# A decoder block on one core: the SSD chunks' buffers, queue and state, one ring of split weights, and y_a's operand

## The chip, the cores and the metric

The kernel runs on one core of a Trainium2 chip. The metric is the device time of one execution in microseconds, the median of several runs. The kernel before took 2039.7 us (three runs: 2036.38, 2039.7 and 2045.04).

In what follows PE is the tensor engine (matmuls), DVE the vector engine, ACT the scalar engine, POOL the GpSimd engine and SP the sync engine, which here only issues DMAs. PSUM is the memory that matmuls write, in banks; SBUF is the memory that the other engines work in.

## The reference

One layer, a sequence of 1024 positions, model width 1024, all in float32:

```
u  = rmsnorm(h)
P  = u @ W_in          # 1024 x 10272: gate_a, gate_s, B_a, C_a, v_a, z, xBC, dt
y_a = (B_a * causal_dwconv3(C_a * v_a)) @ W_a_out
xBC = silu(causal_dwconv4(xBC) + b)          # x (2048), B and C (4 groups x 128 each)
y  = SSD(x, dt, B, C) + d_skip * x           # 32 heads of 64, state 128, chunks of 128
y_s = group_rmsnorm(y * silu(z)) @ W_s_out   # 4 groups of 512
h  = h + (sigmoid(gate_a) * y_a + sigmoid(gate_s) * y_s) @ W_o
v  = rmsnorm(h)
h  = h + (silu(causal_dwconv3(v @ W_1) + b) * (v @ W_3)) @ W_down
out = rmsnorm(h)
```

For one group and one chunk of 128 positions, SSD is: a masked product inside the chunk (C Bᵀ times a decay, times x·dt), plus C times the state at the chunk's start times a decay, and then state = state × (decay of the whole chunk) + Bᵀ(x·dt·decay to the end). There are 4 groups with 8 chunks each, so 32 chunks, and the state is carried over 8 of them.

## The kernel before, in words

**Products.** Each float32 operand is split into a high and a low part (`split`, L146: ACT copies the high part, DVE or POOL subtracts for the low part), and a product adds high×high, high×low and low×high. A product (L248) has 12 matmuls of 128×512. Two column tiles of a weight make a `Pair` (L261), which computes its 2×2 block product with seven products in place of eight. They have fixed names by their operand: b11, b21 (`first`), t1, t2, t3, t4, b22 (`second`); t1 to t4 are sums and differences of weight tiles formed on POOL (L292, L293, L304, L310). The results are put together on DVE (u2, u3 and the drains, L302 to L314).

**Buffers.** Tiles come from rings; an instruction that writes a tile waits until the last reader of the ring's oldest tile is done. Here: raw weights (`load`, L156, SP's queue) 3; split weights `w` 11, and a second ring `wx` of 4 for t4 and b22; t1 to t3 in a ring `t2` of 3; `big` 14 tiles of 128×2048, the operands among them. PSUM has four banks `mm` and four banks `sd`. The products t1, t4 and b22 and all tiles of the SSD take `sd` banks in turn, so whatever is allocated four places later takes the same bank.

**The scratch of `fill_second`** (L207), which transposes rows of the activation and forms the five remaining combinations, are two tiles per row block; they come from the ring `wx`.

**SSD chunks.** `ssd_chunk` (L617) is a generator with eight stages; every finished product advances a clock (`tick`, L324), and the stages of chunk number s are due at 11 + 6s plus the offsets in STAGES (L54). So a chunk starts every six products, between the projections of x, B, C, z, the convolution mixer and the gates. Its steps, with the lines of the profile:

- m: decays loaded through ACT's queue, then exponentials on ACT (L639, L640)
- in: x, B, C of the chunk loaded from DRAM by SP's queue (L633), two buffers
- px, pb, pc (L645, L647, L649): transposes of x and B, and BᵀC, each in a bank of its own; xd, xe, bk and cb are drawn from them (L651, L658, L666, L668); POOL multiplies x by d_skip in place (L662)
- eb, zt: decays and silu(z) loaded by ACT's queue (L680 for zt, one buffer)
- pd, po, pst (L687, L694, L700): the product inside the chunk, C times the state, and the state's increment
- POOL scales the state in place (L702), DVE adds pd (L706), DVE multiplies po by its decay (L708), POOL adds that (L709), DVE adds pst to the state (L716), DVE multiplies by the gate in place, over x (L718)
- ACT squares (L721) and writes y to DRAM out of the buffer of x (L722), DVE sums (L723, L725); PE sums over partitions (pn, L728), DVE forms the mean (yss, L730), POOL the power (yr, L734)

Afterwards `ta_half` (L793) loads y_a's operand through the ring of raw weights in pieces of two tiles and splits them; `y_a` (L807) follows.

**Order.** A scheduler of the framework lays out each engine's instructions in one list ahead of time; each engine runs its list strictly in order. Where an instruction waits, all behind it on that engine wait too, DMA issues on the queues of SP and ACT among them.

Of the kernel before, what the change touches and what calls it, by code (L numbers as in the profile page):

```python
# [15 lines left out]
P = 128  # L16
# [17 lines left out]
NRAW, NW, NWX, NBIG, NB4, NC2, NT2, NROW = 3, 11, 4, 14, 3, 6, 3, 6  # L34
# [19 lines left out]
STAGES = LOAD_M, LOAD_IN, DECAY, TRANS, LOAD_Z, DIAG, SQUARES, NORM = -9, -8, -6, -4, -3, 0, 3, 6  # L54
# [11 lines left out]
def tile_block(  # L66
# [58 lines left out]
    def w2(name, tag="w", dt=F32R):  # L125
        return wp.tile([P, HALF], dt, tag=tag, name=name, bufs=NW if tag == "w" else NWX)
# [24 lines left out]
    def wsplit(v, name, eng=None, tag="w"):  # L151
        hi, lo = w2(f"h_{name}", tag), w2(f"l_{name}", tag)
        split(v, hi, lo, eng)
        return hi, lo
# [5 lines left out]

    ident = const([P, P], "ident")
# [45 lines left out]
    def fill_second(A, vts, name):  # L207

        pts, sls, sm = [], [], []
        for v, t in vts:  # L210
            pts.append(transposed(v, f"{name}{t}", mm_tile))
            sls.append(slice(t * P, (t + 1) * P))

        def piece(nm, i, f):
            return f(f"{nm}_{name}{vts[i][1]}").rearrange("p (k t) -> p k t", k=4)

        def wx(nm):
            return w2(nm, "wx", F32)
# [4 lines left out]
        def whole(c, i, f):  # L223
            o = piece(c, i, f)
# [5 lines left out]
        a11 = [whole("a11", i, c2) for i in both]  # L230
# [5 lines left out]
        s3 = [piece("s3", i, wx) for i in both]  # L236
# [4 lines left out]
        a12 = [whole("a12", i, wx) for i in both]  # L241
# [19 lines left out]
    class Pair:  # L261
# [26 lines left out]
        def operands(self):  # L288
            name, b11 = self.name, self.r1[:, :HALF]
            self.r2 = load(self.src2, f"2{name}")  # L290
            self.t1, self.t2 = t2(f"t1{name}"), t2(f"t2{name}")
            pool.tensor_tensor(self.t1, self.r2[:, :HALF], b11, op=ALU.subtract)  # L292
            pool.tensor_tensor(self.t2, self.r2[:, HALF:], self.t1, op=ALU.subtract)  # L293

        def second(self, d2):
            name, m1, d1 = self.name, self.m1, self.d1
            b21, t1, tb = self.r1[:, HALF:], self.t1, self.t2
            b12, b22 = self.r2[:, :HALF], self.r2[:, HALF:]
# [4 lines left out]
            t3 = t2(f"t3{name}")  # L303
            pool.tensor_tensor(t3, b22, b12, op=ALU.subtract)  # L304
            p = self.prod("s3", t3, "t3")
# [44 lines left out]
    halves = [slice(0, HALF), slice(HALF, SEQ)]  # L350
# [78 lines left out]
    for j in range(0, 4, 2):  # L429
        for t in (4 + j, 5 + j):  # L430
            u_norm(t)
        fill_second(U, [(xs[t], t - 4) for t in (4 + j, 5 + j)], "u")
# [182 lines left out]
    states, stats = {}, {}  # L615

    def ssd_chunk(s):  # L617
# [15 lines left out]
        sp.dma_start(inp, xd_[g][:, 0:6, ts])  # L633
# [45 lines left out]
        zt = ssp.tile([P, 4, P], F32, tag="z", name=f"zt{nm}", bufs=1)  # L679
# [21 lines left out]
        if st is not None and c < NCH - 1:  # L701
            pool.tensor_tensor(  # L702
                heads(st), heads(st),
                cdb[:, q, hsl, cc : cc + 1].to_broadcast([P, HG, HD]), op=ALU.mult,
            )
# [4 lines left out]
        if c < NCH - 1:  # L710
            if st is None:
                st = ssp.tile([P, HALF], F32, tag="st", name=f"st{g}", bufs=1)
                act.copy(st, pst)
                states[g] = st
            else:
                dve.tensor_tensor(st, st, pst, op=ALU.add)  # L716

        dve.tensor_tensor(xt, xt, zt, op=ALU.mult)  # L718
        yield
        sq = eb  # L720
        act.activation(sq, xt.rearrange("p j l -> p (j l)"), AF.Square)  # L721
        act.dma_start(yd[g, c // 4][:, :, hts], xt)  # L722
# [506 lines left out]
```

## Time and profile before

| | |
|---|---|
| median of three runs | 2039.7 us |
| profiled execution | 2035.02 us |
| its span, first to last instruction | 2033.3 us |
| mean granted clock of PE | 0.981 |
| busy: PE, DVE, POOL, ACT | 1933.0, 1390.5, 1309.6, 909.9 us |
| HBM traffic | 166 GB/s over the span |

By stage: the head to 110 us; projections without SSD to 250; projections with the SSD chunks beside them to 960; y_a and the rest of the mixer to 1325; the norm ahead of the FFN to 1420; the up projections of the FFN to 1795; the down projections to the end.

How to read the rows: a line such as `DVE st L716 <- POOL st L702: 68.4, 17, 11.6` says that DVE, at line 716 writing the tile st, sat idle 68.4 us in all, 17 times, at most 11.6 us, until POOL's instruction of line 702 was done. Names have their numbers left out: st is the state of any group, `in` the buffer of x, B and C. A row with `SPq` or `ACTq` is a DMA issue on that engine's queue. The clock column is the share of full speed that PE was granted.

### The profile page before, as it was taken

The numbers are of one execution on the slowest core, as the hardware profiler recorded it, in microseconds if no ns is written. First come the engines' busy times: TensorE is split into PE (matmuls) and PEld (weight loads), VectorE is DVE, ScalarE is ACT, GpSimd is POOL, SyncE is SP. The second block draws the span as 40 slices with busy tenths as digits, with TensorE's granted clock in tenths as the row PEclk, the third lists the DMA queues.
The fourth block names the chain that finished last, engine by engine and source line by source line (L and its number), as shares of the span: only waits on it lengthen the run. The fifth ranks groups of instructions, "written<-read, shape, count | busy, mean of one in ns | idle before, by whom it ended". The sixth has DMA issues, their size and how long they took to land.

```text
span 2033.3 us, 25995 instructions
## 1 busy us (share of the span) xinstructions
PE 1933.0 (95%) x8978; PEld 1578.5 (78%) x8978; DVE 1390.5 (68%) x1588; ACT 909.9 (45%) x1687; POOL 1309.6 (64%) x959
## 2 busy tenths in 40 slices
PE   7899999989999999998999999998999999999998
PEld 6788877767778778776787888876888888887886
DVE  8765996767778767766775724367876677784445
ACT  5364447536636655444333423354433333343434
POOL 7777877766777678676545322367888777753452
PEclk9999999999999999999999999998999999999999
DMA  4252234535444544477998555542332244467664
GB/s 150 62 174 99 104 126 147 169 121 158 161 121 132 184 140 151 109 231 241 325 342 322 194 183 181 166 156 73 130 109 99 91 151 148 156 224 272 211 193 155
DMA packets 184339, 338.46 MB, mean 166 GB/s; under 512 B 19472, under 2 KB 91920, under 8 KB 183184
## 3 DMA queue, kind: packets, MB, share of 16 engines
q1 hardware_dynamic: 122512, 266.53, 39.3%
q10 hardware_dynamic: 61696, 70.27, 11.6%
q8 instruction: 71, 1.16, 0.2%
q14 instruction: 60, 0.49, 0.1%
HBM read 247.34 MB, written 89.41 MB: 166 GB/s over the span
## 4 chain that ended last, share of the span: by engine, by line
PE 63%; DMA 13%; DVE 9%; POOL 7%; issue 5%; ACT 3%; SPq 0%; ACTq 0%; POOLq 0%; DVEq 0%
PE so L255 7%; PE pt2up L255 3%; PE pt4up L255 3%; DMA wd<-in_w_down 3%; PE pt3up L255 3%; PE pb22up L255 3%; PE pb11up L255 3%; PE pt1up L255 3%; PE pb21up L255 3%; PE d L1022 2%; PE d L1024 2%; PE d L1023 2%; PE ya L255 2%; PE pb22xb L255 1%; PE pt4xb L255 1%
## 5 line engine op out<-in xcount | busy, mean ns | idle before, releaser
L536 DVE SCALAR_TENSOR_TENSOR cv<-xbc,scw,cv 128x1024 f32<-128x1024 f32 x72 | 131.9, 1855 | 15.2 <-ACT cv L532 15.2
L639 ACT ACTIVATE m<-m,tk 128x128 f32<-128x128 f32 x256 | 79.2, 390 | 112.1 <-DMA m<-acd 96.1
L536 DVE SCALAR_TENSOR_TENSOR fcv<-fci,fcw,fcv 128x1024 f32<-128x1024 f32 x44 | 77.8, 1769 | 31.4 <-ACT fcv L532 31.4
L149 POOL TENSOR_TENSOR l_ws<-raw_ws,h_ws 128x512 fp32r<-128x512 f32 x32 | 44.9, 1405 | 77.4 <-issue 29.2
L148 ACT CAST h_ws<-raw_ws 128x512 fp32r<-128x512 f32 x64 | 38.5, 621 | 85.5 <-PE so L255 59.6
L255 PE MATMUL so<-yh,h_ws 128*128 128x512 f32 x256 | 70.0, 396 | 4.4 <-ACT h_ws L148 4.4
L149 DVE TENSOR_TENSOR l_ws<-raw_ws,h_ws 128x512 fp32r<-128x512 f32 x32 | 28.0, 880 | 64.0 <-PE so L255 35.0
L255 PE MATMUL so<-yl,h_ws 128*128 128x512 f32 x256 | 69.5, 393 | 0.0
L255 PE MATMUL so<-yh,l_ws 128*128 128x512 f32 x256 | 68.6, 390 | 0.0
L658 ACT ACTIVATE xe<-px,tk 128x64 f32<-128x64 f32 x256 | 55.9, 329 | 25.6 <-DVE xd L651 25.5
L149 POOL TENSOR_TENSOR l_wo<-raw_wo,h_wo 128x512 fp32r<-128x512 f32 x24 | 34.3, 1432 | 50.8 <-ACT h_wo L148 24.9
L292 POOL TENSOR_TENSOR t1up<-raw_2up,raw_1up 128x512 f32<-128x512 f32 x22 | 32.0, 1455 | 53.8 <-DMA raw_2up<-in_w_up 38.5
L716 DVE TENSOR_TENSOR st<-st,pst 128x512 f32<-128x512 f32 x24 | 16.5, 686 | 71.0 <-POOL st L702 68.7
L255 PEld LDWEIGHTS so<-yh,h_ws 128*128 128x128 f32 x256 | 47.8, 189 | 15.4 <-ACT h_ws L148 5.9
L718 DVE TENSOR_TENSOR in<-in,zt 128x512 f32<-128x512 f32 x32 | 44.9, 1404 | 18.8 <-POOL in L709 16.4
L255 PEld LDWEIGHTS so<-yl,h_ws 128*128 128x128 f32 x256 | 48.6, 190 | 10.3
L255 PEld LDWEIGHTS so<-yh,l_ws 128*128 128x128 f32 x256 | 48.3, 189 | 10.2
L1010 DVE TENSOR_TENSOR fcv<-fcv,h 128x1024 f32<-128x1024 f32 x22 | 39.8, 1811 | 23.2 <-ACT fcv L1009 23.2
L148 ACT CAST h_wo<-raw_wo 128x512 fp32r<-128x512 f32 x48 | 29.6, 622 | 56.8 <-PE wo L896 26.8
L895 PE MATMUL wo<-l_wo,mh 128*128 128x512 f32 x128 | 51.2, 400 | 3.2 <-DVE l_wo L149 3.2
L669 DVE TENSOR_TENSOR m<-m,cb 128x1024 f32<-128x1024 f32 x32 | 53.2, 1662 | 0.4
L896 PE MATMUL wo<-h_wo,ml 128*128 128x512 f32 x128 | 50.8, 398 | 0.0
(1060 smaller groups left out, 6664.4 us busy)
## 6 DMA issues: line engine op xcount, KB each, us to landing
m<-acd ACTq DMA_DIRECT2D x32, 512.0 KB, 4.5
raw_ws<-in_w_s_out SPq DMA_DIRECT2D x32, 512.0 KB, 4.7
ssd_in<-cv ACTq DMA_DIRECT2D x24, 512.0 KB, 2.7
in<-ssd_in SPq DMA_DIRECT2D x32, 384.0 KB, 3.9
raw_wo<-in_w_o SPq DMA_DIRECT2D x24, 512.0 KB, 3.5
wd<-in_w_down SPq DMA_DIRECT2D x22, 512.0 KB, 6.1
td<-wd SPq DMA_DIRECT2D x44, 256.0 KB, 4.6
raw_1up<-in_w_up SPq DMA_DIRECT2D x22, 512.0 KB, 3.4
```

The source lines that it names most:

```text
L148: act.copy(hi, v)
L149: (eng or pool).tensor_tensor(lo, v, f32(hi), op=ALU.subtract)
L255: pe.matmul(ps, wt[:, k, :], ct[:, k, :], start=(start and n == 0), stop=(stop and n == 11),)
L536: dve.scalar_tensor_tensor(cv, ci[:, j : j + SEQ], w[:, j : j + 1], cv, op0=ALU.mult, op1=ALU.add)
L639: act.activation(m[:, h, :], m[:, h, :], AF.Relu, bias=a)
L658: act.activation(xe[:, hc], px[:, hc], AF.Copy, scale=tk[:, 2, cc, q, g * HG + h : g * HG + h + 1],)
L669: dve.tensor_tensor(m, m, cb.unsqueeze(1).to_broadcast([P, HG, P]), op=ALU.mult)
L718: dve.tensor_tensor(xt, xt, zt, op=ALU.mult)
L895: pe.matmul(pss[t], mh, wl, start=False, stop=False)
L896: pe.matmul(pss[t], ml, wh, start=False, stop=k == NK - 1)
L1022: pe.matmul(ps, aa[0][:, ts], bb[0], start=k == 0, stop=False)
L1023: pe.matmul(ps, aa[0][:, ts], bb[1], start=False, stop=False)
```

## The change

It has three parts.

1. *SSD tiles.* The load of x, B, C moves from SP's queue to ACT's and is due one product earlier, at the same one as the load of m (LOAD_IN −9). The multiply by the gate writes into zt instead of the buffer of x, and the square and the write to DRAM read zt, which gets a second buffer. pb and pc share one bank. The state is no longer scaled in place ahead of its add: after each add POOL scales the new state by the next chunk's decay into a tile of its own, sn, and the next add reads sn.
2. *Rings.* One ring of 13 split weights takes the place of 11 and 4. t3 is formed with t1 and t2, in `operands`. The scratch of `fill_second` comes from a small pool (at the head) or is the row block's own two halves (ahead of the FFN).
3. *y_a's operand* is loaded into a tile of 128×2048 of its own in two pieces, no longer through the ring of raw weights.

```diff
-NRAW, NW, NWX, NBIG, NB4, NC2, NT2, NROW = 3, 11, 4, 14, 3, 6, 3, 6
+NRAW, NW, NBIG, NB4, NC2, NT2, NROW = 3, 13, 14, 3, 6, 3, 6
...
-STAGES = LOAD_M, LOAD_IN, DECAY, TRANS, LOAD_Z, DIAG, SQUARES, NORM = -9, -8, -6, -4, -3, 0, 3, 6
+STAGES = LOAD_M, LOAD_IN, DECAY, TRANS, LOAD_Z, DIAG, SQUARES, NORM = -9, -9, -6, -4, -3, 0, 3, 6
...
-        return wp.tile([P, HALF], dt, tag=tag, name=name, bufs=NW if tag == "w" else NWX)
+        return wp.tile([P, HALF], dt, tag="w", name=name, bufs=NW)
...
-    def fill_second(A, vts, name):
+    def fill_second(A, vts, name, own=None):
...
-        def wx(nm):
-            return w2(nm, "wx", F32)
+        def spare(i, n):
+
+            t = vts[i][0][:, halves[n]] if own is None else own.tile(
+                [P, HALF], F32, tag="own", name=f"own{n}_{name}{vts[i][1]}", bufs=4
+            )
+            return t.rearrange("p (k t) -> p k t", k=4)
...
-            tag = "wx" if nm in ("t4", "b22") else "w"
-            product(ps, self.A[c], wsplit(v, f"{nm}{name}", eng, tag))
+            product(ps, self.A[c], wsplit(v, f"{nm}{name}", eng))
...
-            self.t1, self.t2 = t2(f"t1{name}"), t2(f"t2{name}")
+            self.t1, self.t2, self.t3 = (t2(f"t{i}{name}") for i in (1, 2, 3))
             pool.tensor_tensor(self.t1, self.r2[:, :HALF], b11, op=ALU.subtract)
             pool.tensor_tensor(self.t2, self.r2[:, HALF:], self.t1, op=ALU.subtract)
+            pool.tensor_tensor(
+                self.t3, self.r2[:, HALF:], self.r2[:, :HALF], op=ALU.subtract
+            )
...
-        sp.dma_start(inp, xd_[g][:, 0:6, ts])
+        act.dma_start(inp, xd_[g][:, 0:6, ts])
...
-        pb = sd_tile(f"pb{nm}")[:, :P]
+        pbc = sd_tile(f"pb{nm}")
+        pb, pc = pbc[:, :P], pbc[:, P : 2 * P]
         pe.transpose(pb, bt, ident)
-        pc = sd_tile(f"pc{nm}")[:, :P]
...
-        zt = ssp.tile([P, 4, P], F32, tag="z", name=f"zt{nm}", bufs=1)
+        zt = ssp.tile([P, 4, P], F32, tag="z", name=f"zt{nm}", bufs=2)
...
-        if st is not None and c < NCH - 1:
-            pool.tensor_tensor(
-                heads(st), heads(st),
-                cdb[:, q, hsl, cc : cc + 1].to_broadcast([P, HG, HD]), op=ALU.mult,
-            )
         dve.tensor_tensor(xt, xt, tiles(pd), op=ALU.add)
         if st is not None:
             dve.tensor_tensor(eb, po, eb, op=ALU.mult)
             pool.tensor_tensor(xt, xt, tiles(eb), op=ALU.add)
...
-                dve.tensor_tensor(st, st, pst, op=ALU.add)
-
-        dve.tensor_tensor(xt, xt, zt, op=ALU.mult)
+                dve.tensor_tensor(st, decayed[g], pst, op=ALU.add)
+        if c < NCH - 2:
+
+            q1, c1 = (c + 1) // 2, (c + 1) % 2
+            decayed[g] = sn = ssp.tile([P, HALF], F32, tag="sn", name=f"sn{nm}", bufs=1)
+            pool.tensor_tensor(
+                heads(sn), heads(st),
+                cdb[:, q1, hsl, c1 : c1 + 1].to_broadcast([P, HG, HD]), op=ALU.mult,
+            )
+
+        dve.tensor_tensor(zt, xt, zt, op=ALU.mult)
         yield
         sq = eb
-        act.activation(sq, xt.rearrange("p j l -> p (j l)"), AF.Square)
-        act.dma_start(yd[g, c // 4][:, :, hts], xt)
+        act.activation(sq, zt.rearrange("p j l -> p (j l)"), AF.Square)
+        act.dma_start(yd[g, c // 4][:, :, hts], zt)
...
+            tt = (extra_tile if hf else big_tile)(f"ta{hf}{q}")
             for k in range(0, 4, 2):
-                raw = load(
-                    tad[:, 4 * q + k : 4 * q + k + 2, hf * HALF : (hf + 1) * HALF],
-                    f"ta{hf}{q}{k}",
-                ).rearrange("p (k t) -> p k t", k=2)
-                split(raw, hi[:, k : k + 2, :], lo[:, k : k + 2, :], dve)
+                ks = slice(k, k + 2)
+                sp.dma_start(tt[:, ks, :], tad[:, 4 * q + k : 4 * q + k + 2, halves[hf]])
+                split(tt[:, ks, :], hi[:, ks, :], lo[:, ks, :], dve)
```

The lists of the engines move with it. In the rows below a name ends in group, chunk and a running number (`px2_4` is of group 2, chunk 4; `pt1cv4` is the product t1 of the pair cv4). Most lines of the new kernel have numbers 3 or 4 higher (the product is L259).

PE, where chunk 4 of group 2 is transposed, before:

```order
L645 MATMUL px2_4_6540<-ident_75,in2_4_6414 128x128 x4
L647 MATMUL pb2_4_6545<-ident_75,in2_4_6414 128x128
L255 MATMUL pb21cv4_6568<-ua12h_135,h_b21cv4_6569 128x512 x4
L255 MATMUL pb21cv4_6568<-ua12l_136,h_b21cv4_6569 128x512 x4
L255 MATMUL pb21cv4_6568<-ua12h_135,l_b21cv4_6570 128x512 x2
L649 MATMUL pc2_4_6547<-in2_4_6414 128x128
L255 MATMUL pb21cv4_6568<-ua12h_135,l_b21cv4_6570 128x512 x2
L255 MATMUL pt1cv4_6604<-us1h_312,h_t1cv4_6605 128x512 x4
```

and now:

```order
L648 MATMUL px2_4_6537<-ident_75,in2_4_6395 128x128 x4
L651 MATMUL pb2_4_6542<-ident_75,in2_4_6395 128x128
L652 MATMUL pb2_4_6542<-in2_4_6395 128x128
L259 MATMUL pb21cv4_6564<-ua12h_135,h_b21cv4_6565 128x512 x4
L259 MATMUL pb21cv4_6564<-ua12l_136,h_b21cv4_6565 128x512 x4
L259 MATMUL pb21cv4_6564<-ua12h_135,l_b21cv4_6566 128x512 x4
L259 MATMUL pt1cv4_6604<-us1h_312,h_t1cv4_6605 128x512 x4
```

pc stood inside the product b21, ten matmuls behind pb, in the bank of chunk 3's pst; now it stands right behind pb, in pb's bank, and t1's product is what takes the bank of that pst.

POOL, around the state of chunk 3, before:

```order
L734 TENSOR_TENSOR yr2_0_6050<-yss2_2_6461,nhalf_80 128x1
L293 TENSOR_TENSOR t2cv5_6828<-raw_2cv5_6825,t1cv5_6827 128x512
L304 TENSOR_TENSOR t3cv5_6904<-raw_2cv5_6825 128x512
L702 TENSOR_TENSOR st2_5864<-st2_5864,cdb_226 128x512
L709 TENSOR_TENSOR in2_3_6202<-in2_3_6202,eb2_3_6390 128x512
L149 TENSOR_TENSOR l_b11cv5_6776<-raw_1cv5_6772,h_b11cv5_6775 128x512
```

and now:

```order
L739 TENSOR_TENSOR yr2_0_6046<-yss2_2_6457,nhalf_80 128x1
L295 TENSOR_TENSOR t1cv5_6823<-raw_2cv5_6821,raw_1cv5_6768 128x512
L296 TENSOR_TENSOR t2cv5_6824<-raw_2cv5_6821,t1cv5_6823 128x512
L707 TENSOR_TENSOR in2_3_6179<-in2_3_6179,eb2_3_6388 128x512
L718 TENSOR_TENSOR sn2_3_6480<-st2_5859,cdb_226 128x512
L149 TENSOR_TENSOR l_t4cv4_6702<-t2cv4_6599,h_t4cv4_6701 128x512
L297 TENSOR_TENSOR t3cv5_6825<-raw_2cv5_6821 128x512
```

The scaling stood ahead of the add into `in`, and t3 ahead of both; now the add comes first, then the scaling into sn, then an l_ tile and t3. On DVE, in the same place, the state's add (L713) is now followed directly by the multiply by the gate (L723), where a drain of a product (L314) and a split stood between the two.

ACT, where chunk 2's y is written, before (chunk 4's `in` is loaded by SP's queue, L633):

```order
L721 ACTIVATE eb2_2_6174<-in2_2_5998 128x512
L722 DMA yd20_101<-in2_2_5998 512x1x128
L680 DMA zt2_3_6393<-ssd_in2_86 128x4x128
L658 ACTIVATE xe2_3_6346<-px2_3_6335,tk_225 128x64 x8
L675 DMA eb2_3_6390<-ead_109 64x4x128 x2
```

and now:

```order
L726 ACTIVATE eb2_2_6172<-zt2_2_6175 128x512
L727 DMA yd20_101<-zt2_2_6175 512x1x128
L636 DMA in2_4_6395<-ssd_in2_86 128x6x128
L546 ACT_TABLE_LOAD
L546 ACTIVATE cv15_6285<-cv15_6285 128x1024
L683 DMA zt2_4_6589<-ssd_in2_86 128x4x128
```

The load of `in` for chunk 4 stands right behind the write of chunk 2's y, and the load of zt is a chunk further ahead.

More of the change, by code (lines that the diff above doesn't have):

```diff
@@ L123, in t2, with w2 @@
         return scr.tile([P, HALF], F32, tag="t2", name=name, bufs=NT2)
-    def w2(name, tag="w", dt=F32R):
-        return wp.tile([P, HALF], dt, tag=tag, name=name, bufs=NW if tag == "w" else NWX)
+    def w2(name, dt=F32R):
+        return wp.tile([P, HALF], dt, tag="w", name=name, bufs=NW)
     def row(name, w=2 * P):
@@ L149, in split, with wsplit @@
         (eng or pool).tensor_tensor(lo, v, f32(hi), op=ALU.subtract)
-    def wsplit(v, name, eng=None, tag="w"):
-        hi, lo = w2(f"h_{name}", tag), w2(f"l_{name}", tag)
+    def wsplit(v, name, eng=None):
+        hi, lo = w2(f"h_{name}"), w2(f"l_{name}")
         split(v, hi, lo, eng)
@@ L159, in load @@
         return raw
+    halves = [slice(0, HALF), slice(HALF, SEQ)]
     ident = const([P, P], "ident")
@@ L215, in piece, with whole @@
             return f(f"{nm}_{name}{vts[i][1]}").rearrange("p (k t) -> p k t", k=4)
-        def wx(nm):
-            return w2(nm, "wx", F32)
+        def spare(i, n):
[3 more added lines that the diff above has]
+            return t.rearrange("p (k t) -> p k t", k=4)
         def put(c, i, val, eng=dve):
             split(val, A[c][0][:, :, sls[i]], A[c][1][:, :, sls[i]], eng)
-        def whole(c, i, f):
-            o = piece(c, i, f)
+        def whole(c, i, o):
             hi, lo = (f32(t[:, :, sls[i]]) for t in A[c])
@@ L229, in fill_second @@
         both = range(len(vts))
-        a11 = [whole("a11", i, c2) for i in both]
+        a11 = [whole("a11", i, piece("a11", i, c2)) for i in both]
         s1 = [piece("s1", i, c2) for i in both]
@@ L235, in fill_second @@
             put("s1", i, s1[i])
-        s3 = [piece("s3", i, wx) for i in both]
+        s3 = [spare(i, 0) for i in both]
         for i in both:
@@ L240, in fill_second @@
             dve.tensor_tensor(s3[i], a11[i], pts[i][0], op=ALU.subtract)
-        a12 = [whole("a12", i, wx) for i in both]
+        a12 = [whole("a12", i, spare(i, 1)) for i in both]
         for i in both:
@@ L297, in second @@
             b21, t1, tb = self.r1[:, HALF:], self.t1, self.t2
-            b12, b22 = self.r2[:, :HALF], self.r2[:, HALF:]
+            b22 = self.r2[:, HALF:]
             p5 = self.prod("s1", t1, "t1", sd_tile)
@@ L302, in second @@
             dve.tensor_tensor(u2, m1, p, op=ALU.add)
-            t3 = t2(f"t3{name}")
-            pool.tensor_tensor(t3, b22, b12, op=ALU.subtract)
-            p = self.prod("s3", t3, "t3")
+            p = self.prod("s3", self.t3, "t3")
             u3 = c2(f"u3{name}")
@@ L349, in tile_block @@
     td = dram.tile([KF, 4, P, HALF], F32, name="td")
-    halves = [slice(0, HALF), slice(HALF, SEQ)]
     QT = 2 * P
@@ L431, in tile_block @@
             u_norm(t)
-        fill_second(U, [(xs[t], t - 4) for t in (4 + j, 5 + j)], "u")
+        fill_second(U, [(xs[t], t - 4) for t in (4 + j, 5 + j)], "u", cur["row"])
         p = Pair(U, w_in[GA + j], w_in[GA + j + 1], f"g{GA + j}", cur["row"])
@@ L613, in tiles @@
         return t.rearrange("p (j l) -> p j l", j=4)
-    states, stats = {}, {}
+    states, decayed, stats = {}, {}, {}
     def ssd_chunk(s):
@@ L711, in ssd_chunk @@
             if st is None:
-                st = ssp.tile([P, HALF], F32, tag="st", name=f"st{g}", bufs=1)
+                st = states[g] = ssp.tile([P, HALF], F32, tag="st", name=f"st{g}", bufs=1)
                 act.copy(st, pst)
-                states[g] = st
             else:
-                dve.tensor_tensor(st, st, pst, op=ALU.add)
-        dve.tensor_tensor(xt, xt, zt, op=ALU.mult)
+                dve.tensor_tensor(st, decayed[g], pst, op=ALU.add)
[7 more added lines that the diff above has]
+        dve.tensor_tensor(zt, xt, zt, op=ALU.mult)
         yield
         sq = eb
-        act.activation(sq, xt.rearrange("p j l -> p (j l)"), AF.Square)
-        act.dma_start(yd[g, c // 4][:, :, hts], xt)
+        act.activation(sq, zt.rearrange("p j l -> p (j l)"), AF.Square)
+        act.dma_start(yd[g, c // 4][:, :, hts], zt)
         dve.tensor_tensor(sq[:, : 2 * P], sq[:, : 2 * P], sq[:, 2 * P :], op=ALU.add)
```

## The prediction

> **What bounds the kernel now.** I read the table of stages first (the columns are stretch and length in us, then busy time and instruction count of PE, PE's weight loads, DVE, ACT and POOL, then PE's granted clock, the DMA share and GB/s).
>
> ```profile
> PE 1933.0 (95%) x8978; PEld 1578.5 (78%) x8978; DVE 1390.5 (68%) x1588; ACT 909.9 (45%) x1687; POOL 1309.6 (64%) x959
> ...
> 110.00:250.00 140.00, 140.00 (x620) 115.95 (x619) 97.70 (x92) 68.31 (x102) 105.88 (x77) 1.00 0.35 118
> 250.00:960.00 710.00, 662.93 (x3339) 531.91 (x3338) 523.18 (x632) 377.59 (x871) 508.44 (x386) 0.97 0.51 155
> ...
> 1325.00:1420.00 95.00, 82.23 (x344) 66.25 (x344) 67.80 (x78) 44.48 (x86) 70.00 (x50) 0.91 0.33 111
> 1420.00:1795.00 375.00, 375.00 (x1657) 310.49 (x1656) 278.69 (x270) 139.16 (x201) 303.45 (x209) 1.00 0.37 129
> ```
>
> PE is the bound, with 95% of the span. In the first projections (110 to 250) and in the FFN (1420 to 1795) it never stops and has its full clock: nothing can be won there, only lost. The SSD stage (250 to 960), where the chunks run beside the projections, is different: PE stands for 710 − 662.9 = 47 us and has a clock of 0.97, which is worth 0.03 × 710 = 21 us more. A second look at this stage, at the product line alone, says the same:
>
> ```profile
> 250.00:960.00 710.00, 579.25 (x2322) 0.97 0.51 155
> ```
>
> In the first projections a matmul costs 140/620 = 0.226 us; 2322 of them would take 524 us, and they took 579. The 55 us are slow and interrupted products, the clock's 21 among them. I take 47 + 21 and some 20 of small gaps, about 88 us, as all that there is to win in this stage. Next, who made PE wait there (waiter, releaser, us in total, times, longest):
>
> ```profile
> PE pst L700 <- DVE yss L730: 13.1, 6, 3.1
> PE pc L649 <- DVE st L716: 11.1, 7, 5.5
> PE pt1ba L255 <- DVE st L716: 4.7, 1, 4.7
> PE po L694 <- DVE gt L314: 3.0, 1, 3.0
> PE pb22z L255 <- DVE cb L668: 3.0, 1, 3.0
> PE pc L649 <- DVE cc L312: 2.6, 2, 2.4
> PE px L645 <- DMA in<-ssd_in: 2.4, 1, 2.4
> PE pc L649 <- DVE gt L309: 1.1, 1, 1.1
> ```
>
> All but one of these wait for DVE, though DVE is busy for only 523 of 710 us. So DVE isn't short of time; it is late. The waits of DVE and of the queues name why:
>
> ```profile
> DVE st L716 <- POOL st L702: 68.4, 17, 11.6
> DVE eb L723 <- ACT eb L721: 20.4, 14, 4.9
> DVE in L718 <- POOL in L709: 15.2, 12, 4.1
> ...
> ACT m L639 <- DMA m<-acd: 94.3, 22, 9.4
> ACT eb L721 <- DVE in L718: 49.2, 19, 5.6
> ...
> SPq L633 <- DMA yd<-in: 229.8, 27, 18.9
> ```
>
> The add of the state (L716) waits 68.4 us for POOL to scale the state (L702). One chunk in full, in order of start (start, duration, instruction, idle time before it):
>
> ```profile
> 562.78 0.69 DVE L708 TENSOR_TENSOR eb<-po,eb 128x512 f32<-128x512 f32 x1 [1.03 <-PE po L694]
> ...
> 566.16 1.29 POOL L293 TENSOR_TENSOR t2ba<-raw_2ba,t1ba 128x512 f32<-128x512 f32 x1
> 567.41 0.55 POOL L734 TENSOR_TENSOR yr<-yss,nhalf 128x1 f32<-128x1 f32 x1
> 567.93 1.29 POOL L304 TENSOR_TENSOR t3ba<-raw_2ba 128x512 f32<-128x512 f32 x1
> ...
> 569.17 1.06 POOL L702 TENSOR_TENSOR st<-st,cdb 128x512 f32<-128x512 f32 x1
> 570.18 1.27 POOL L709 TENSOR_TENSOR in<-in,eb 128x512 f32<-128x512 f32 x1
> 570.26 0.69 DVE L716 TENSOR_TENSOR st<-st,pst 128x512 f32<-128x512 f32 x1 [6.79 <-POOL st L702]
> 571.00 0.49 PE L649 MATMUL pc<-in 128*128 128x128 f32 x2 [0.64 <-DVE st L716]
> 571.48 1.77 DVE L718 TENSOR_TENSOR in<-in,zt 128x512 f32<-128x512 f32 x1 [0.54 <-POOL in L709]
> ```
>
> POOL has the scaling queued behind t2, the power of yr and t3 of the next pair. DVE stands 6.8 us with everything else behind it, and PE's pc waits because its bank is pst's.
>
> **The change part by part.** The sum stands against the profiled execution, 2035.0 us (span 2033.3 and 1.7 around it); the median of the runs shown is 2039.7, 4.7 above it, and the forecast adds that back.
>
> *State scaled a step ahead, one bank less.* The add now needs no POOL work of its own chunk, and pc shares pb's bank, so it no longer waits for the add. What takes pst's bank is t1's product, which stands some 2.7 us of products later. Gone: 11.1 + 4.7, and of the bank waits 2.6 and 1.1 under pc about 2 of 3.7: **−18 us**. The waits left, for yss, gt and cb (13.1 + 3.0 + 3.0, about 19, and some of 1 us or less, which I put at 2), are DVE running late. DVE's idle 68.4 doesn't all vanish: the multiply by the gate still needs POOL's add (L709), and in the new order it stands right behind the state's add on DVE. In the chunk above POOL would do that add ahead of t3, of the scaling, and of one l_ tile that now come later, so 1.29 + 1.06 + 1.29 = 3.6 us sooner (the l_ tile taken at t3's duration): it would end near 567.8 where it ended at 571.45. The state's add would run at 564.5 to 565.2, and the multiply wait some 2.6 us. So 6.8 + 0.5 us of waiting becomes 2.6, a bit over a third, and of 68.4 + 15.2 = 84 about 30 stay. As 54 of 84 go, I let half of those 21 go: **−10 us**; ends 0 (these waits come from yss standing behind drains of products, which don't move) and −21.
>
> ```profile
> L716 DVE TENSOR_TENSOR st<-st,pst x24: 670/687/689, 321.6 to 972.7; 128x512 f32<-128x512 f32 x24
> L702 POOL TENSOR_TENSOR st<-st,cdb x24: 1037/1050/1569, 320.0 to 971.6; 128x512 f32<-128x512 f32 x24
> L709 POOL TENSOR_TENSOR in<-in,eb x28: 1257/1289/2276, 321.0 to 997.6; 128x512 f32<-128x512 f32 x28
> L718 DVE TENSOR_TENSOR in<-in,zt x32: 677/1754/1803, 299.8 to 999.4; 128x512 f32<-128x512 f32 x32
> L633 SPq DMA_DIRECT2D in<-ssd_in x32: 370/377/1125, 278.9 to 954.9; - x32
> ```
>
> These are the pieces (ns, least, median, most). The floor of the new wait is 1.29 − 0.69 = 0.6 us for each of 24 chunks, 14 us in all, if POOL is free at once. The multiply takes 0.68 us at its least and mostly 1.75, beside POOL's work; were it always 1.75, that is 32 × (1.754 − 1.404, its mean of 44.9/32) = 11 us more on DVE, which has 187 idle. The Trainium skill (SBUF — State Buffer, Who interferes with whom) says that a DVE operation with two SBUF inputs and a GpSimd operation that reads SBUF shut each other out; the two levels of L718 agree, and by that rule the scaling, which DVE used to wait for and which now runs beside its multiply, costs up to 24 × 1.05 = 25 us of DVE time. If all of it fell on the waits, 29 us of them would go and not 54, the term would be −7, and the sum 3 us higher.
>
> *Clock.* Fewer stalls, fewer slow spells. In proportion to the waits, of which 28 of 47 go, it would be 12 of the 21: **−12 us**; ends 0 and −21.
>
> *x, B, C loaded by ScalarE's queue.* 32 issues of 0.377 us leave SP and come to ACT: 12 us. They no longer hold up SP, whose queue stood 229.8 us at this line with the weight loads of the projections behind it. In the new order the issue stands directly behind the write of yd, whose data and whose release of the buffer are both done by then (the buffer is free at the multiply, as y goes over the gate), so ACT has no new wait. ACT's order also has four more table loads:
>
> ```profile
> L640 ACT ACT_TABLE_LOAD x11 | 14.1, 1283 | 1.4 <-issue 1.3
> ```
>
> 5 us. ACT is busy for 378 of 710, so these 17 us are hidden: **0**; without that cover they are +17. PE's wait of 2.4 for the load goes or stays: −1.
>
> *One ring of 13 split weights* in place of 11 + 4, and t3 formed early. A product takes two tiles, so a pair's seven products find room for 6.5 where they found (11 + 4)/2 = 7.5, of which the four could serve two products of the seven only. Splits may still run six products ahead of PE, 6 × 12 matmuls × 0.226 = 16 us. **0**; ends 0 and +8 (the FFN stage goes from no idle to 2%).
>
> *y_a's operand apart.* Its tiles are no longer the three raw buffers that weights use.
>
> ```profile
> PE ya L255 <- ACT h_wa L148: 2.6, 1, 2.6
> ACT tah L148 <- DMA raw_ta<-tad: 11.1, 3, 8.2
> ...
> DMA to landing us min/median/max: 4.4/7.3/10.2
> ...
> 990.85 1.07 PE L255 MATMUL pb21g<-ua12h,l_b21g 128*128 128x512 f32 x4
> 1005.50 1.18 PE L255 MATMUL ya<-tah,h_wa 128*128 128x512 f32 x4
> ```
>
> At best −3, PE's wait there. The last load now waits for a big tile whose last reader is pb21 of the last gate pair, which ended some 14 us before y_a began; such a load took 4.4 to 10.2 us to land, and its two halves of the split follow. Just in time: **0**, ends −3 and +10. The scratch of the second fill gets its own tiles; it stands at the head and in 1325 to 1420, where PE idles 12.8 us: **0**, ends ±4.
>
> Sum: −18 − 10 − 12 − 1 = −41, and I keep **+4** back for the costs at 0, whose far ends are nearly all positive. That is −37: 1998 for the profiled execution, and 2002.7, say **2003 us**, as the median.
>
> **The rivals.** *The wait moves to the multiply.* DVE now waits for L709 in place of L702, and does so ahead of the drains of products; if POOL stays as late as the 6.8 us above (its queue is 508 of 710 busy), DVE gains little. Then only the direct terms come, −18 and a little clock, less 4 for costs: about −16, 2024. For it: the new order puts the multiply ahead of a drain that it stood behind. Against: POOL's add is three operations earlier.
>
> *No change.* The direct terms come, but 16 us are paid back by the ring, the load of ta or the changed order around the decays (ACT's 94.3 at L639): 2035 to 2045. For it: pst's wait for yss, the largest, is not touched.
>
> *Slower: ACT inherits SP's wait.* SP stood 229.8 us in 27 waits, 8.5 us each, for the buffer of `in`. If the buffer were as late for ACT, ACT would be held in its own order: 377.6 + 229.8 + 94.3 + 49.2 = 751 us against 710, and the stage would end about 41 later, at 2080. It decides from a wait of (710 − 378 − 143)/30 = 6.3 us a chunk. Against: by the order, everything that the issue needs is done when ACT comes to it; SP waited because it asked for the buffer early. For: ACT serves the splits for all products, so any error here falls on PE at once.
>
> **How the numbers follow.** The forecast has 0.60, the moved wait 0.17, no change 0.12, slower 0.11. Half a per cent, some 10 us, is about what a measurement of this kernel can tell from no change: faster means below 2029.5, slower above 2049.9. Faster takes the forecast's 0.58 and the moved wait's 0.15, 0.73; same 0.15; slower 0.12. The likeliest case by itself reaches from 2040 − 70 (every term at its good end: 18 + 21 + 21 + 6, and a few gaps) to 2040 − 18 (the direct terms alone): 1970 to 2022. The range takes in the moved wait and the edge of no change: 1970 to 2042.
>
> **What would show it.** Right: in the changed trace the state's add waits for PE alone, POOL's line of the scaled state releases nobody, pc has no waits, the SSD stage shrinks by 30 to 45 us with a clock near 0.985, and the multiply's wait for POOL is 20 to 40 us in all. The moved wait: that wait is above 60. The inherited wait: the issue of `in` on ACT's queue stands for microseconds, and ACT's idle time is there. The ring: h_ or l_ tiles waiting for PE right ahead of a PE wait in the FFN, now at no idle. Wrong at its root: PE's 47 us stay though the state's add is early; then they never came from POOL's lateness.

## The result, and the profile after

The changed kernel takes 2050.8 us (median of 11 runs, 2043.6 to 2059.8) where the kernel before takes 2035.8 in as many: a ratio of 1.0076, 95% interval 1.0054 to 1.0098. It is 15 us slower, where 37 us faster was forecast, and outside the range (1970 to 2042). Its profiled execution has a span of 2048.4 us, 15.1 more than before.

Where the 15.1 us come from can be read from the first and last starts of two tiles (line, then least, median and most ns, then the first and last start). Before:

```profile
L645 PE MATMUL px<-ident,in x128: 270/272/300, 283.3 to 972.4; 128*128 128x128 f32 x128
L255 PE MATMUL ya<-tah,h_wa x128: 389/391/504, 1005.5 to 1188.5; 128*128 128x512 f32 x128
```

and after:

```profile
L648 PE MATMUL px<-ident,in x128: 270/272/445, 290.8 to 994.8; 128*128 128x128 f32 x128
L259 PE MATMUL ya<-tah,h_wa x128: 388/393/632, 1026.5 to 1207.5; 128*128 128x512 f32 x128
```

To the first px the changed kernel is 7.5 us late; from there to the first product of y_a it takes 735.7 us where it took 722.2 (13.5 more); from y_a on it takes 1021.9 where it took 1027.8 (5.9 less). So the stage that was to win 41 us lost 13.5. The windows of the changed kernel, to be read against those of before:

```profile
250.00:960.00 710.00, 653.48 (x3279) 526.33 (x3279) 532.57 (x621) 375.90 (x854) 511.75 (x378) 0.97 0.51 150
...
1420.00:1795.00 375.00, 374.03 (x1643) 309.53 (x1644) 298.42 (x272) 143.72 (x203) 310.26 (x209) 1.00 0.36 123
```

PE is idle for 56.5 us in the SSD stage (47 before), the clock is 0.97 as before, and in the FFN it is idle for 1 us (0 before). Who made PE wait in this stage (250 to 975):

```profile
PE pst L703 <- DVE yss L735: 11.7, 7, 3.2
PE pb22z L259 <- DVE cb L671: 11.0, 2, 9.5
PE pd L690 <- DVE m L672: 7.3, 5, 3.7
PE px L648 <- DMA in<-ssd_in: 6.0, 1, 6.0
PE po L697 <- DVE pr L313: 4.5, 2, 4.2
PE pb L651 <- DVE st L713: 3.2, 1, 3.2
PE pb22xb L259 <- DVE cb L671: 3.1, 2, 2.6
```

The rows of pc are gone, as forecast: pc waits for nobody (pb, ahead of it, waits once for the state's add, 3.2 us). In their place stand rows of cb, and of m, which is multiplied by cb: 11.0 + 3.1 + 7.3, with a smaller one of 0.8, 22 us. Before, cb and m had 3.9. Why cb is late stands in the rows of DVE and ACT:

```profile
DVE zt L723 <- POOL in L707: 48.4, 21, 5.3
DVE cb L671 <- ACT bk L669: 35.8, 10, 13.2
...
DVE st L713 <- PE pst L703: 6.9, 7, 2.7
...
ACT m L642 <- DMA m<-acd: 118.1, 25, 12.7
```

The state's add waits for PE alone now, and POOL's scaling releases nobody: that part does what it was meant to do. But cb, which DVE reads out of the bank that pb and pc now share, waits 35.8 us for bk, which ACT reads out of the same bank. Before there was no such row: cb waited 0.9 us, for pc. The longest case in order of time (the changed kernel, 500 to 508 us):

```profile
500.17 2.46 ACT L642 ACTIVATE m<-m,tk 128x128 f32<-128x128 f32 x8 [9.99 <-DMA m<-acd]
503.16 1.28 ACT L643 ACT_TABLE_LOAD   x1
504.45 1.06 ACT L643 ACTIVATE m<-m 128x1024 f32<-128x1024 f32 x1
505.92 0.26 ACT L669 COPY bk<-pb 128x128 f32<-128x128 f32 x1
...
506.21 0.29 DVE L671 TENSOR_TENSOR cb<-pb,tri 128x128 f32<-128x128 f32 x1 [13.15 <-ACT bk L669]
...
506.56 1.65 PE L259 MATMUL pb22z<-us4h,h_b22z 128*128 128x512 f32 x3 [9.46 <-DVE cb L671]
507.02 2.00 DVE L672 TENSOR_TENSOR m<-m,cb 128x1024 f32<-128x1024 f32 x1
```

ACT stands 10 us for the load of m, does its exponentials with a table load, and only then copies bk, which takes 0.26 us. cb has waited 13 us for that copy, and PE 9.5 us for cb, since the product b22 takes the bank next. ACT's wait for m was there before (94.3 us), but cb had no wait for ACT then; the shared bank lets it through. This case is the extreme, though. Eight of cb's waits are over 1 us, and in the other seven ACT is at work for most of the wait or all of it, on what stands ahead of bk in its list: m's exponentials, table loads, an activation of z and casts of splits. In the changed kernel every one of the 32 cb waits for its bk, and all 32 start after it; before, 12 of 32 started ahead of it. The Trainium skill (PSUM — Partial Sum Buffer, PSUM bank collisions raise a hardware error) says why such a wait is put in: two engines must not touch one bank at once, and two readers of different columns count too. The trace agrees in that no bk and cb overlap (before, with banks apart, one pair of 32 does); the page gives no price for it.

### The profile page after: what moved, and what is told of

The parts are those of the page before. It is cut to its first block, busy times and chain, and to the rows that moved or that the text cites. A ratio compares the mean times of both kernels' runs of the same rounds, so it can differ in the third digit from the quotient of the medians.

```text
span 2048.4 us, 25977 instructions
## 1 busy us (share of the span) xinstructions
PE 1937.7 (95%) x8978; PEld 1583.8 (77%) x8978; DVE 1437.8 (70%) x1588; ACT 920.0 (45%) x1691; POOL 1333.5 (65%) x959
## 4 chain that ended last, share of the span: by engine, by line
PE 64%; DVE 12%; DMA 9%; issue 6%; POOL 5%; ACT 4%; ACTq 1%; SPq 0%; POOLq 0%; DVEq 0%
PE so L259 9%; PE pt3up L259 3%; PE pt2up L259 3%; PE pt4up L259 3%; PE pb22up L259 3%; DMA m<-acd 3%; PE pt1up L259 3%; PE d L1026 3%; PE d L1027 3%; PE pb21up L259 3%; PE pb11up L259 3%; PE d L1028 3%; PE ya L259 2%; DVE cv L539 2%; PE pb21xb L259 1%
## 5 line engine op out<-in xcount | busy, mean ns | idle before, releaser
L539 DVE SCALAR_TENSOR_TENSOR fcv<-fci,fcw,fcv 128x1024 f32<-128x1024 f32 x44 | 85.5, 1943 | 27.9 <-ACT fcv L535 27.8
L723 DVE TENSOR_TENSOR zt<-in,zt 128x512 f32<-128x512 f32 x32 | 46.5, 1453 | 49.3 <-POOL in L707 49.2
L259 PE MATMUL so<-yh,h_ws 128*128 128x512 f32 x256 | 68.9, 391 | 1.0 <-DVE ga L822 1.0
L259 PE MATMUL so<-yl,h_ws 128*128 128x512 f32 x256 | 68.6, 389 | 0.0
L259 PE MATMUL so<-yh,l_ws 128*128 128x512 f32 x256 | 68.5, 389 | 0.0
L149 POOL TENSOR_TENSOR l_wa<-raw_wa,h_wa 128x512 fp32r<-128x512 f32 x16 | 30.4, 1902 | 49.4 <-ACT h_wa L148 32.3
L149 DVE TENSOR_TENSOR l_wo<-raw_wo,h_wo 128x512 fp32r<-128x512 f32 x24 | 24.3, 1015 | 52.1 <-ACT h_wo L148 26.6
L259 PEld LDWEIGHTS so<-yh,h_ws 128*128 128x128 f32 x256 | 47.7, 188 | 10.9 <-ACT h_ws L148 1.3
L259 PEld LDWEIGHTS so<-yl,h_ws 128*128 128x128 f32 x256 | 48.1, 188 | 10.0
L259 PEld LDWEIGHTS so<-yh,l_ws 128*128 128x128 f32 x256 | 48.1, 188 | 10.0
L898 PE MATMUL wo<-h_wo,mh 128*128 128x512 f32 x128 | 49.9, 391 | 1.2 <-DVE h L903 1.2
```

The costliest lines, as they stand in the source:

```text
L149: (eng or pool).tensor_tensor(lo, v, f32(hi), op=ALU.subtract)
L259: pe.matmul(ps, wt[:, k, :], ct[:, k, :], start=(start and n == 0), stop=(stop and n == 11),)
L539: dve.scalar_tensor_tensor(cv, ci[:, j : j + SEQ], w[:, j : j + 1], cv, op0=ALU.mult, op1=ALU.add)
L898: pe.matmul(pss[t], mh, wh, start=k == 0, stop=False)
```

## The experiments

The ratios are against the kernel before on the same chip; the expectations are as written ahead of the runs. The kernel before itself has a median of 2035.8 us beside the changed kernel and of 2026 to 2032 on the chips of the experiments, so times, and lengths in profiles, of different runs compare less well than ratios.

| kernel | what it is | ratio | 95% interval |
|---|---|---|---|
| e1_own_banks | changed, pc in a bank of its own | 0.9992 | 0.9978 to 1.0007 |
| e2_bk_dve | changed, bk copied by DVE | 1.0003 | 0.9987 to 1.0019 |
| e3_cb_first | changed, cb ahead of bk | 1.0037 | 1.0023 to 1.0050 |
| e4_in_sp | changed, load of x, B, C on SP's queue | 1.0078 | 1.0052 to 1.0104 |
| b1_bank | before, pc in pb's bank | 1.0102 | 1.0087 to 1.0117 |
| b4t_ring_t3 | before, one ring, early t3 | 0.9999 | 0.9984 to 1.0013 |
| b5_ta | before, y_a's operand apart | 0.9980 | 0.9971 to 0.9990 |
| b6_t3 | before, early t3 | 0.9989 | 0.9975 to 1.0004 |
| e5_no_state | e1, state scaled in place as before | 1.0005 | 0.9993 to 1.0017 |
| e6_mul_pool | e1, multiply by the gate on POOL | 1.0056 | 1.0037 to 1.0075 |
| e7_add_dve | e1, add of the state's part on DVE | 0.9970 | 0.9960 to 0.9981 |
| e8_no_add | e1, that add left out | 0.9935 | 0.9915 to 0.9955 |
| e9_add_dve_no_state | e7, state scaled in place | 0.9938 | 0.9915 to 0.9960 |
| e10_few | before, early t3, y_a's operand apart, that add on DVE | 0.9957 | 0.9938 to 0.9975 |
| e11_add_dve_in_sp | e7, load of x, B, C on SP's queue | 0.9991 | 0.9975 to 1.0007 |

### The shared bank

Banks apart again, all else as changed:

```diff
-        pbc = sd_tile(f"pb{nm}")
-        pb, pc = pbc[:, :P], pbc[:, P : 2 * P]
+        pb = sd_tile(f"pb{nm}")[:, :P]
         pe.transpose(pb, bt, ident)
+        pc = sd_tile(f"pc{nm}")[:, :P]
```

> The changed kernel with pc in a PSUM bank of its own again; all else as changed. Theory A (the shared bank): in the changed kernel cb, which DVE reads out of the bank, waits for bk, which ACT reads out of the same bank (DVE stood 35.8 us for it between 250 and 975 us), and PE stood 15.7 us for cb and 7.3 us for m behind it. With banks apart these 23 us fall below 4, the wait of cb on bk is not in the trace, and the time falls by 15 to 25 us, to 2026 to 2036. Rival B (the queue: x, B, C on ACT's queue and the reordered ACT are what costs): the time stays within 6 us of the changed kernel's 2051. Rival C (the ring of split weights): the same as B.

One bank, but both readers on one engine:

```diff
-        act.copy(bk, pb)
+        dve.tensor_copy(bk, pb)
```

> The changed kernel with the shared bank kept, but bk copied out of it by DVE, directly ahead of cb, in place of ACT: the two readers of the bank are on one engine. Theory A: the wait on another engine is gone and the time falls as with banks apart, by 15 to 25 us less 32 copies of some 0.2 us of DVE, so 12 to 25 us. If a shared bank costs something else than this wait (a bank that comes free later for the product behind it), less than 8 us comes back. Rivals B and C: within 6 us of 2051.

One bank, and the lines of bk and cb exchanged, so that bk waits for cb:

> The changed kernel with the shared bank kept, and cb written ahead of bk in the program, so that bk (ACT) waits for cb (DVE) and not the other way round. Theory A: DVE's wait of 35.8 us is gone, ACT has a new one for cb; PE needs bk only at pst, so PE's waits for cb and m fall below 8 us and the time falls by 8 to 22 us. If the direction does not matter (ACT is as costly to hold as DVE), it stays within 6 us of 2051.

The kernel before with the first diff reversed, nothing else:

> The kernel before with one part of the change alone: pc in pb's bank. The state is scaled as before, two rings, SP's queue. Theory A (the shared bank costs through cb waiting for ACT's bk): the wait of cb on bk appears with 20 us or more, PE's waits of pc for the state's add (11.1 + 4.7 us) vanish, PE waits for cb and m by some 20 us; the time is 0 to 20 us above before, likely 8. If sharing the bank only cost in company with the other parts, the time is below before by some 10 us, since the waits of pc go.

All four go with the shared bank. With banks apart the kernel is at 0.9992, so this one part is worth 0.84%, 17 us. With bk on DVE the bank is still shared and all of it comes back but 0.1% (1.0003): what costs is the wait between the two engines, not the bank. With the order turned round, about half comes back (1.0037): cb no longer waits for bk, PE's waits for m and cb fall to 2.9 us, and no row has ACT waiting for cb, as ACT comes later anyway. In their place PE waits for xe, which ACT draws from the transposed x (e3_cb_first, 250 to 970 us):

```profile
PE pb22z L259 <- ACT xe L661: 10.7, 4, 4.7
```

Whether this row is all of the half that stays is not shown. And alone, in the kernel before, the shared bank costs 1.02%, 21 us, just above the top of what was expected, though it takes away pc's waits for the state's add. The rows of b1_bank (250 to 975 us):

```profile
PE pb22z L255 <- DVE cb L668: 11.3, 4, 4.1
...
PE pb22xb L255 <- DVE cb L668: 5.2, 1, 5.2
...
DVE cb L668 <- ACT bk L666: 30.6, 11, 5.4
```

are the same wait as in the changed kernel, without any of its other parts. In the longest case here ACT isn't waiting for a load; it is busy ahead of bk the whole time (b1_bank, 671 to 677 us):

```profile
671.04 1.28 ACT L640 ACT_TABLE_LOAD   x1
672.34 1.06 ACT L640 ACTIVATE m<-m 128x1024 f32<-128x1024 f32 x1
...
673.41 1.28 ACT L543 ACT_TABLE_LOAD   x1
...
674.71 1.06 ACT L543 ACTIVATE cv<-cv 128x1024 f32<-128x1024 f32 x1
675.67 0.60 ACT L148 CAST h_t3xb<-t3xb 128x512 fp32r<-128x512 f32 x1
...
676.18 0.26 ACT L666 COPY bk<-pb 128x128 f32<-128x128 f32 x1
...
676.47 0.29 DVE L668 TENSOR_TENSOR cb<-pb,tri 128x128 f32<-128x128 f32 x1 [5.41 <-ACT bk L666]
```

So it is the place of bk in ACT's list that cb inherits, with or without a wait for m's load ahead of it. PE's own rows for cb and m are not the price either: they come to 22 us in the changed kernel, 18 in b1_bank, 11 in e4_in_sp below and 10 in e2_bk_dve, and the four lose 0.76, 1.02, 0.78 and 0.03%.

### The queue

```diff
-        act.dma_start(inp, xd_[g][:, 0:6, ts])
+        sp.dma_start(inp, xd_[g][:, 0:6, ts])
```

with LOAD_IN −8 again.

> The changed kernel with x, B, C loaded by SP's queue again, one product later as before; all else as changed. Theory A (shared bank alone): the wait of cb on bk stays above 25 us and the time within 6 us of 2051. Rival B (the queue): PE's wait of 6.0 us for the load and DVE's wait for ACT's bk shrink since ACT no longer holds the issue (the longest issue took 3.6 us), and the time falls by 8 to 20 us.

Nothing moves (1.0078 beside 1.0076): cb's wait for bk is 23.7 us, a little under the 25 expected, PE's wait for the load 5.7, and SP's queue stands 187.6 us for the buffer again. Since the bank's wait could have hidden a difference, the same was done later without it:

> The changed kernel with banks apart and the add on DVE (0.9970), with x, B, C loaded by SP's queue, one product later, as before. In the changed kernel with the shared bank the queue made no difference (1.0078 against 1.0076), where the bank's wait may have hidden one. If ACT's queue costs its 32 issues and its place ahead of splits, this is 5 to 12 us faster, 0.991 to 0.9945; if SP's queue holds the weights up, it is slower than 0.999; the prediction's 0 for the queue means 0.995 to 0.999.

There SP's queue is 0.2% slower than ACT's (0.9991 beside 0.9970; the intervals overlap by less than 0.1%, and the two were measured on different chips). So ACT's queue costs nothing and may bring 4 us. The rival in which ACT inherits SP's wait did not happen; ACT's issues of this load took 0.4 to 3.6 us, with a median of 0.64 where 0.377 was counted, and only two of the 32 took over 1 us.

### The ring, t3 and y_a's operand

Each part by itself in the kernel before, with the lines of the change:

> The kernel before with the second part of the change alone: one ring of 13 split weights, t3 formed early, own scratch for the second fill. The prediction has 0 with ends 0 and +8, and the head and the norm ahead of the FFN at 0 with ends -4 and +4. Rival C: the ring holds splits up, the time is 8 to 20 us above before.

> The kernel before with t3 formed early, together with t1 and t2, and nothing else. In the ring part alone (2028 beside 2027 before) the wait of the state's add for POOL was 46 us where it was 68, the head 5 us longer and the FFN 5 us longer. If early t3 is what brings POOL's scaling forward, that wait is below 55 us here, with the time within 8 us of before, and the FFN is as short as before (430 us from the last product of the mixer to the last of the up projections); the 5 us then belong to the ring.

> The kernel before with the third part of the change alone: y_a's operand loaded into tiles of its own. The prediction has 0 with ends -3 and +10. In the changed kernel the way from the start of y_a to the down projections took 801.5 us where it took 806.3 before, and from the last gate product to y_a it was 7 us shorter; if this part is what did that, the time is 5 to 10 us below before.

The ring with early t3 is level (0.9999), early t3 alone level to slightly faster (0.9989), y_a's operand apart 0.2% faster, 4 us. The lengths of the stages in the profiled executions, by the same rows as above (to the first px; from there to the first ya; to the last wo with a high part; to the last pb22 of the up projections):

| | head | SSD | mixer | up |
|---|---|---|---|---|
| before | 283.3 | 722.2 | 371.3 | 432.9 |
| b5_ta | 283.0 | 711.9 | 368.2 | 432.4 |
| b6_t3 | 284.1 | 709.3 | 369.3 | 433.8 |
| b4t_ring_t3 | 288.7 | 711.1 | 366.5 | 435.4 |
| b1_bank | 283.3 | 740.3 | 362.5 | 433.6 |
| changed | 290.8 | 735.7 | 364.1 | 435.4 |
| e1_own_banks | 287.8 | 725.8 | 359.4 | 435.5 |
| e7_add_dve | 289.8 | 713.5 | 358.0 | 433.8 |

The head's 5 us belong to the ring with its own scratch, not to early t3; some 3 of them are PE's wait for the first load of x, B, C, which is 5.0 to 6.0 us in the kernels with the ring and 2.2 to 2.5 in those without (why is open). In the up projections the kernels with the ring are up to 2.6 us longer in their profiles than before, within the 0 to 8 of the prediction. The expectation's 55 us for the wait of the state's add came out at 56.9 with early t3 alone and 46.4 with the ring, where before has 68.4; but b5_ta, which has neither, has 61.9, so t3 by itself may do little. The table shows something else: b5_ta leaves the SSD's code as it is, yet its stage is 10 us shorter than in the profile of before, with PE idle for 40.3 us (47.1) and a clock of 0.99 (0.97). In the other direction, b1_bank's mixer is 9 us shorter than before's, though its edit lies in the chunks. Ten us in one stage of one profile is thus no more than two chips or executions can differ by; which of the two it is, the runs don't tell. The rows of before for pc are 11.1 and 4.7; those of b5_ta (250 to 970 us) are

```profile
PE pc L649 <- DVE st L716: 6.9, 5, 2.7
...
PE pt1ba L255 <- DVE st L716: 2.6, 1, 2.6
```

and 6.8 and 2.6 in b6_t3. The ring alone, without early t3, wasn't tried on the chip.

### The state scaled ahead, and DVE's waits for POOL

From e1_own_banks, the state scaled in place again (the lines of the kernel before, on POOL ahead of DVE's adds):

> The changed kernel with banks apart (measured 2032, level with before) and the state scaled in place, ahead of its own add, as before; the rest as changed. My prediction gave the scaling ahead and the bank together -28 and -12 through the clock. If that gain is there and other parts eat it, this kernel is 20 to 40 us slower than 2032, at 2052 to 2072. If DVE's wait for POOL merely moved (in the kernel with banks apart DVE still stands 52 us at the multiply for POOL's add), it stays within 8 us of 2032.

The scaling ahead is worth 0.13% (0.9992 beside 1.0005), 3 us, and the intervals overlap; PE's idle time between 250 and 970 is no smaller with it (53.4 us beside 48.9). DVE's rows for POOL in e5_no_state (250 to 970 us):

```profile
DVE st L719 <- POOL st L705: 41.5, 14, 5.6
DVE zt L721 <- POOL in L712: 22.0, 20, 1.8
```

and in e1_own_banks:

```profile
DVE zt L723 <- POOL in L707: 52.0, 20, 4.9
```

63.5 us became 52.0. DVE no longer meets POOL at the state's add, but one operation later, at the multiply, which needs POOL's add into the same tile: the wait moved. Three kernels ask what it is worth, each with one line of e1_own_banks changed (in this order e6_mul_pool, e7_add_dve and e8_no_add):

```diff
-        dve.tensor_tensor(zt, xt, zt, op=ALU.mult)
+        pool.tensor_tensor(zt, xt, zt, op=ALU.mult)
...
-            pool.tensor_tensor(xt, xt, tiles(eb), op=ALU.add)
+            dve.tensor_tensor(xt, xt, tiles(eb), op=ALU.add)
...
-            pool.tensor_tensor(xt, xt, tiles(eb), op=ALU.add)
```

> The changed kernel with banks apart (2032, level with before), and the multiply by the gate on POOL in place of DVE, so that DVE never waits for POOL's add (52.0 us at the multiply with banks apart, 83.6 us at both places before). Theory D (DVE's waits for POOL set PE's waits, as predicted): DVE gets 52 us of waiting and 46 us of work back, PE's idle time of some 50 us in the SSD stage falls by 15 us or more, the time by 15 to 35 us. Theory E (DVE has slack, and PE's waits come from where single instructions stand in DVE's list): the time stays within 8 us of the kernel with banks apart, or POOL with 42 us more is late with low parts and it grows.

> The changed kernel with banks apart, and the add of the part from the state (28 of them, 1.29 us on POOL) on DVE, so that the multiply behind it waits for DVE alone. DVE loses 52 us of waiting and gains some 28 x 0.69 to 1.75 = 19 to 49 us of work; POOL loses 37 us of work. Theory D: time 10 to 25 us lower. Theory E: within 8 us of the kernel with banks apart.

> The changed kernel with banks apart, with the add of the part from the state left out altogether (the output lacks C times the carried state): neither POOL nor DVE does it, and the multiply waits for nobody on POOL. This is the ceiling of what any cure of that wait can bring. Theory D: 15 to 40 us below the kernel with banks apart. Theory E: less than 8 us.

Neither theory came out whole. With the add gone from both engines, the ceiling, the time falls by 0.57%, 11.6 us: between D's 15 and E's 8. With the add on DVE it falls by 0.22%, 4.5 us, which E allows. With the multiply on POOL it grows by 0.64%: DVE then meets the same lateness a step further on,

```profile
DVE eb L728 <- ACT eb L726: 71.6, 23, 10.1
```

where e1_own_banks has 28.3 in that row. That alone doesn't explain the loss, since e7_add_dve has 52.4 in it and is faster; the 46 us of work that POOL took on may be the rest, and no run separates the two. So 52 us of DVE's waiting, with 28 of POOL's operations on top, are worth 11.6 us of time, about a fifth (by the two intervals some 6 to 17 us). Last, the scaling in place where nothing else on DVE waits for POOL:

> The changed kernel with banks apart and the add of the part from the state on DVE (0.9970 of before), with the state scaled in place ahead of its own add, as before. With the add on POOL, the scaling ahead was worth 0.9992 against 1.0005, some 3 us. If it was worth so little because DVE met POOL again at the multiply (moved wait), it is worth clearly more here, where nothing else on DVE waits for POOL: this kernel is 8 to 20 us slower than with the scaling ahead, 1.001 to 1.007 of before. If DVE's wait for the scaling had slack in any case, the two are within 5 us: 0.995 to 0.9995.

It is no slower but faster than e7 (0.9938 beside 0.9970; the intervals meet at 0.9960), below both ranges of the expectation, though DVE has its wait for the scaling back:

```profile
DVE st L719 <- POOL st L705: 25.9, 10, 4.0
```

So the moved wait is not all of the reason that the scaling ahead brings nothing; also where it had no second meeting with POOL, it brought nothing. Why it should cost is open. The few parts by themselves, in the kernel before:

> The kernel before with three things only: t3 early (0.9989 alone), y_a's operand apart (0.9980 alone) and the add of the part from the state on DVE. Two rings, SP's queue, own bank for pc and the state scaled in place stay. If the pieces add up, 0.9989 x 0.998 x some 0.998 = 0.995, 10 us below before, since the 5 us in the head and the 5 us in the FFN of the single ring are not paid. If the wait for the scaling decides, DVE stands 50 us for it and the time is 0.997 or more.

0.9957, 9 us faster, near the sum of the parts, though DVE stands 48.5 us for the scaling. e9_add_dve_no_state, with banks apart, one ring, ACT's queue, y_a's operand apart, the state scaled in place and the add on DVE, has the lowest time of the kernels that compute everything, 2012.9 us, 0.62% under the kernel before, and beats both. Between it and e10_few the intervals don't decide.

## Why the prediction was wrong

**The step that failed** is the first term, "State scaled a step ahead, one bank less": it counted the waits that the shared bank takes away (−18) and not the one that it adds. That pb and pc have readers on two engines stood in the kernel (bk on ACT, cb on DVE), that m's exponentials come ahead of bk on ACT stood in the list of steps, and one way that ACT is late stood in a row that the prediction quotes for another purpose, ACT's 94.3 us for m. Put together they say: once cb must follow bk, ACT's lateness reaches DVE and, through the bank, PE. What the runs showed in place of the −18: cb waits for bk 35.8 us in the changed kernel and 30.6 in b1_bank, and the time grows by 17 us in the changed kernel (e1_own_banks takes it away) and by 21 alone (b1_bank). The prediction had ACT's 94.3 as rival material only, for the queue and the decays.

**The −18 of direct waits.** pc's rows vanished from the trace of the changed kernel, where one wait of 3.2 us for the state's add is left, now at pb. But the size was taken from one execution: 15.8 us of waits for the state's add there, 9.5 in b5_ta, whose chunks are the same, on another chip. And with banks apart the time is level with before, not 18 us lower: PE's idle time between 250 and 970 is 53 us in e1_own_banks and 47 in the profile of before. Where one row goes, others stand. Rows of e1_own_banks that before doesn't have:

```profile
PE pb22g L259 <- DVE gt L316: 7.4, 1, 7.4
PE pd L690 <- ACT xe L661: 5.7, 1, 5.7
PE pt1cv L259 <- DVE pr L318: 5.5, 2, 4.1
```

The first stands in b4t_ring_t3 too (6.4 us), where the state is scaled in place, so not all of them took the place of pc's. The prediction's sign for being wrong at its root, PE's 47 us staying though the state's add is early, is what e1_own_banks shows. What it drew from that sign, that these us never came from POOL's lateness, is not shown either way: without POOL's add (e8_no_add) PE stands 35.9 us, but b6_t3, which has that add, stands 40.1 on the same chip.

**The −10 for DVE's lateness** rested on 54 of 84 us of DVE's waits going. Over the whole change 84 became 48.4, so 35 went; in the pair that differs by the scaling alone 11.5 of 63.5 went (the multiply's wait was put at 30 and measured 52.0; 48.4 in the changed kernel). The rate, 10 us for 54, was near the 11.6 for 52 of e8_no_add, which also takes 28 operations from POOL; as it was a half that no row gave, that is luck. It was the quantity that was mis-sized, and the rival "the wait moves to the multiply", put at 0.17, named where it went, though its sign, a wait above 60, did not come either. Its own 2024 failed by the bank too: the direct terms on which it rested are not there.

**The −12 of the clock** was tied to the waits and did not come: 0.97 in both. The tie itself isn't borne out from one run to another: between 250 and 960 e6_mul_pool has 53.3 us of idle PE at a clock of 0.99, e10_few 39.6 at 0.97.

**SBUF.** The 25 us of DVE time that the prediction worked out by the Trainium skill's rule (SBUF — State Buffer, Who interferes with whom) did not come at the multiply: its busy total went from 44.9 to 46.5 us (48.6 in e1_own_banks). Its two levels are still there (0.69 and 1.76 us), so the trace agrees with the rule and not with that price; a third level of 1.52 us, 12 of the 32 in the changed kernel, is not explained by any run. The 3 us that the prediction took off for this case were too few by its own rate: 29 us for 54 make of −10 about −5, not −7.

**What held:** the queue at 0 (e4_in_sp, and at most 4 us of gain in e11), the ring between 0 and 8 in the FFN, y_a's operand just past the good end of its −3 to +10 (−4), the state's add waiting for PE alone, pc without waits. The head's ±4 for the scratch was +5 in the ring's profile.

**The range** lay wrong because its slow side had one mechanism, the inherited wait of the queue at 0.11, and no bound for what a shared bank can add. From rows it could have had one: cb behind bk, with ACT up to 9.4 us late 22 times and m's exponentials and a table load on top.

## What to carry to other kernels

When two tiles are put into one PSUM bank, list who reads each: readers on two engines are put in order, and the more punctual one inherits the other's waits; keep both readers on one engine, or the banks apart. A wait on an engine that is not the bound has no fixed price (here about a fifth of it reached the time), so its removal can't be costed by its own length, nor by the row that appears next (52.4 us in e7_add_dve, which is faster): it has to be tried. And take the size of waits of a few microseconds from more than one execution.

## What the runs showed that I had not expected

A copy of 0.26 us made a 9.5 us stop of PE, and 17 to 21 us of time in all, by order alone. Moving work off the engine that waits made things slower (e6_mul_pool, 1.0056, with DVE 18 us less busy and 46 us of work moved to POOL), and doing POOL's work on the busier DVE made them faster (e7_add_dve, 0.9970): DVE does that add in some 0.7 us where POOL takes 1.29, and no engine has to be waited for. Scaling the state a chunk ahead, the part with DVE's longest wait behind it, made no difference that could be told from nothing with POOL's add in the way, and none for the better without it.
